# Sums of x for a Strassen product, read from x's copy in memory; one gate pair in place of two single gates; GELU's cubic factor in one pass

## The chip, the core and the metric

The kernel runs on one core of one Trainium2 chip. The metric is the time of one execution in microseconds of the device; lower is better. PE is the matrix engine, DVE the vector engine, ACT the engine of activation functions, POOL the general one; SP only issues transfers here, in the order of its program. Every engine works through a list of instructions that was fixed when the kernel was built.

## The reference

One step of a decoder layer, for 512 prompt tokens and 64 sample tokens, in fp32, D = 2048:

```
proj = x @ w_in + b_in                       # split into the branches' inputs and gates
y_s5 = gelu(s5(u));  y_s5 *= sigmoid(y_s5 @ w_glu + b_glu)
br_s5   = (y_s5 * silu(s5_z)) @ p_s5
br_gla  = (gla(q, k, v, a_low) * silu(gla_z)) @ p_gla
br_conv = (conv(ca, cb) * silu(cz)) @ p_conv
g_s5, g_gla, g_conv = split(sigmoid(gates))
out = (g_s5 * br_s5 + g_gla * br_gla + g_conv * br_conv) @ w_o
h = alpha * x + out;  h = h + sigmoid(h @ w_pg) * (p @ w_pe);  return layer_norm(h)
```

and the new states of the three branches. The S5 branch is a diagonal complex state-space model over 1024 channels. `gates` is 3 x 2048 columns wide: 48 columns of 128.

## The kernel before

All tensors lie transposed, features on partitions and the 576 tokens along the free axis. Each fp32 factor is split into a high part and a low part, both of which the matrix engine takes at full speed, and a product is made of three matmuls: high by high, high by low, low by high. The split is an ACT copy (high) and a DVE subtraction (low, L89). x is kept as 16 tiles `xh[k]` and 16 tiles `xl[k]`, 128 features each. All working tiles come from 71 slots of 128x576, called `sl`.

The input projection is a list of jobs. A *single job* is one column of 128 outputs: 16 k-tiles x 3 products x 2 halves of the tokens = 96 matmuls of 128x288 (L443). A *pair job* makes two columns by Strassen's scheme in Winograd's form: 7 products of 8 k-tiles x 3 matmuls, 168 in all (L472), and DVE and ACT join them. Two single jobs have 192. A pair's products take X's parts A11, A12, A22 and four sums S1 to S4 of x's quarters; with a = x[k] and b = x[k+8] (first half of the tokens 0, second 1):

```
S3 = a0 - a1;  S1 = a1 - b1;  S2 = S1 - a0;  S4 = b0 + S2
```

Order of the products: A11, S1, S2, S4, S3, A12, A22. The second one accumulates in the PSUM tile `aux`, the first and third in `mm`.

Order of the jobs: 8 columns of S5's input u, the column of a_low, then NFILL = 10 gates as single jobs, then the pairs (47), and so on. S5's work on its 8 blocks and the making of the sums run beside the first jobs as generators: each is stepped when it has credit, which a job's progress gives. When the column a_low is done, `make_forms` is started; it waits till 24 slots are free (10 once S5 is done), and makes the sums of one k after another from 16 adds of 128x576 (a = xh + xl, b likewise), subtractions and splits. The first pair needs all of them. A scheduler then fixes each engine's order by simulated times; it moves instructions of different generators past each other.

Of an S5 block the following is needed here. Its kernel `kd` is stored (L964) and loaded again in another layout by 16 DMAs (L980); the scan's input comes from PE (L998), the scan runs on DVE; `s5_out` joins both on PE (L1053 and L1057, the latter with the tiles loaded from kd), applies GELU and stores y by 8 DMAs (L1071). GELU is u times sigmoid of 1.596 u (1 + 0.044715 u^2): Square on ACT, factor and +1 (`ts`) and product (`mul`) on DVE, Sigmoid on ACT, product.

After each of the first eight gates, `x_out` writes two k-tiles of x to memory, `xd`: SP stores `xh[k]` (L1704) and POOL adds `xl[k]` to it by an accumulating DMA (L1705). x is needed there near the end of the layer, for alpha * x.

The file's line numbers are those of the profile of before; the changed file's are 10 or 11 higher from `make_forms` on.

Of the kernel before, what the change touches and what calls it, by code (L numbers as in the profile page):

```python
# [8 lines left out]
F32 = mybir.dt.float32  # L9
F32R = mybir.dt.float32r  # L10
I32 = mybir.dt.int32
AF = mybir.ActivationFunctionType
OP = mybir.AluOpType
# [13 lines left out]
UK = 8  # L27
# [10 lines left out]
TCK = dict(schedule_with_timeline_sim=True)  # L38
PRE, BLK_WAIT = 2, 4
OUT_WAIT, B_WAIT = 4, 2  # L40
NFILL = 10
AHEAD, PREP = 12.9, 6.5
RESERVE, BLOCK_SLOTS = 3, 13

# [1 line left out]
class K:  # L46
# [569 lines left out]
    def make_forms(self):  # L616

        S = {f: ([None] * UK, [None] * UK) for f in ("S1", "S2", "S3", "S4")}
        self.s3, self.stiles = [], []
        for k in range(UK):  # L620
            while len(self.free_slots) < (10 if "s5" in self.done else 24):
                yield None
            a, b, c = self.alloc(), self.alloc(), self.alloc()
            j = k % 2
            if j == 0:
                d, e = self.alloc(), self.alloc()
            cs = slice(j * H, j * H + H)
            self.add(a, self.xh[k].bitcast(F32), self.xl[k].bitcast(F32))
            self.add(b, self.xh[k + 8].bitcast(F32), self.xl[k + 8].bitcast(F32))
            self.sub(c[:, :H], a[:, H:], b[:, H:])  # L630
            self.sub(c[:, H:], c[:, :H], a[:, :H])
            yield 2.1
            self.add(d[:, cs], b[:, :H], c[:, H:])
            self.sub(e[:, cs], a[:, :H], a[:, H:])
            self.free(a, b)
            hi, lo = self.split(c)
            self.stiles += [hi, lo]
            self.free(c)
            for z, f in enumerate(("S1", "S2")):
                for t, p in zip((hi, lo), S[f]):  # L640
                    p[k] = t[:, z * H:(z + 1) * H]
            yield 1.5
            if j:
                hi, lo = self.split(d)
                self.stiles += [hi, lo]
                self.free(d)
                for z in range(2):
                    for t, p in zip((hi, lo), S["S4"]):
                        p[k - 1 + z] = t[:, z * H:(z + 1) * H]
                self.s3.append(e)  # L650
                yield 0.7
        for k in range(UK):
            for p, x in zip(S["S3"], (self.xh, self.xl)):
                p[k] = x[k][:, H:]
        x = (self.xh, self.xl)
        S["A11"] = tuple([t[:, :H] for t in p[:8]] for p in x)
        S["A12"] = tuple([t[:, :H] for t in p[8:]] for p in x)
        S["A22"] = tuple([t[:, H:] for t in p[8:]] for p in x)
        self.forms = S
        self.done.add("forms")  # L660
        yield 0.1
# [380 lines left out]
    def s5_out(self, b, st):  # L1042

        nc = self.nc
        hs = st.pop(("hs", b))
        U, cl, G, L = st.pop(("op", b))
        for _ in range(OUT_WAIT):
            yield
        p = self.two()
        for jj in range(4):  # L1050
            o = (jj // 2) * 512 + (jj % 2) * 144
            for pt in range(2):
                nc.tensor.matmul(p[:, o:o + 144], cl[pt][:, jj * 144 + 16:jj * 144 + 144], hs[pt][:, jj * 144:jj * 144 + 144],  # L1053
                                 start=pt == 0, stop=False)
            for h in range(2):
                gg = 2 * jj + h
                nc.tensor.matmul(p[:, o + h * 72:o + h * 72 + 72], L[gg // 4][:, (gg % 4) * 128:(gg % 4) * 128 + 128],  # L1057
                                 U[:, gg * 72:gg * 72 + 72], start=False, stop=h == 1,
                                 skip_group_check=h == 0)
        self.free(U, *cl, *L)  # L1060
        yield
        u, t = self.alloc(), self.alloc()
        self.act(self.s2(u), self.v2(p))
        self.act(self.s2(t), self.v2(p), AF.Square)
        self.ts(t, t, 0.044715, 1.0)
        self.mul(t, t, u)
        self.act(t, t, AF.Sigmoid, scale=2.0 * math.sqrt(2.0 / math.pi))
        self.mul(u, u, t)
        dst = self.yd[0, b].rearrange("(g c) (s n) -> s c g n", g=8, s=8)
        for s in range(8):  # L1070
            nc.sync.dma_start(dst[s], u[16 * s:16 * s + 16].rearrange("c (g n) -> c g n", g=8))  # L1071
        self.free(t)
        self.stored(u)
        yield 2.0
# [551 lines left out]
    def build(self):  # L1626
# [40 lines left out]
        def fill(n):  # L1667
            for _ in range(n):
                gate_one(*gates.popleft())
# [33 lines left out]
        def x_out(k):  # L1703
            self.pin(nc.sync.dma_start(self.xd[k], self.xh[k].bitcast(F32)))  # L1704
            nc.gpsimd.dma_start(self.xd[k], self.xl[k].bitcast(F32), accum_op=OP.add)  # L1705
# [3 lines left out]
        for n in range(8):  # L1709
            c = OFF["s5_u"] + n * 128  # L1710
            self.job(w_in, c, X, lambda ps, n=n: self.s5_store_u(n, ps))

        self.job(w_in, OFF["a"], X, evac_a, dual=3)
        for j in range(NFILL):
            fill(1)
            if j < 8:
                self.jobs[-1] = self.jobs[-1][:5] + (lambda j=j: (x_out(2 * j), x_out(2 * j + 1)),) + self.jobs[-1][6:]

        ys, yg, yz, yc, G, P = ([None] * 8, [None] * 8, [None] * 8, [None] * 8, [None] * 8, [])

# [589 lines left out]
```

## Time and profile before

| | |
|---|---|
| median of 3 runs | 2279.99 us (2278.43 to 2282.17) |
| profiled execution | 2280.14 us, span of the core 2278.1 us |
| mean granted clock of PE | 0.992 |
| PE busy | 2234.5 us (98%) |
| DVE busy | 1795.0 us (79%) |
| ACT busy | 1041.9 us (46%) |
| POOL busy | 69.3 us (3%) |
| first pair's first matmul | 338.25 us after the span's start |

The engines' busy times overlap, so each is to be read against the span alone. A wait stands in brackets at a row of a timeline: how long the engine was idle ahead of it, and what ended that. SP has no busy time; its rows are the issues of transfers, and a row's length is the time for issuing.

### The profile page before, as it was taken

Reading aid. Unit: us, or ns where it says so; the run is one execution under the profiler, and the core shown is the slowest. Engines: PE = TensorE matmul, PEld = TensorE weight load, DVE = VectorE, ACT = ScalarE, POOL = GpSimd, SP = SyncE. Lnnn points to the kernel's source line nnn. Section 1 sums busy time; section 2 is a strip of 40 time slices with the busy share of each in tenths; the row PEclk is TensorE's granted clock in tenths of the full one; section 3 lists DMA queues with packets and bytes.
Section 4 is the critical chain, followed back from the end, with each engine's and each line's share of the span. In section 5 each row is a group of like instructions: output and inputs, shape, how many; then the busy total and the mean of one; then the engine's idle time right before and its main releaser. Section 6 shows DMA issues by size and latency. Waiting matters only on the chain.

```text
span 2278.1 us, 44359 instructions
## 1 busy us (share of the span) xinstructions
PE 2234.5 (98%) x16892; PEld 2192.4 (96%) x16892; DVE 1795.0 (79%) x3417; ACT 1041.9 (46%) x2058; POOL 69.3 (3%) x121
## 2 busy tenths in 40 slices
PE   8998999999999999999999999999999999999998
PEld 7998999999999999999999999999989999999997
DVE  6977797999898999899989789856653777774556
ACT  4444445454545545545454556553432334453221
POOL 0000000000000000000000000000110000000000
PEclk9999999999999999999999999999999999999998
DMA  7567763434434444534444467856887444464322
GB/s 218 137 143 170 183 163 103 122 116 143 137 116 131 121 134 118 146 113 144 124 137 125 122 208 259 257 164 198 277 222 216 125 135 143 152 207 130 96 85 84
DMA packets 430005, 348.86 MB, mean 153 GB/s; under 512 B 51198, under 2 KB 368314, under 8 KB 429776
## 3 DMA queue, kind: packets, MB, share of 16 engines
q1 hardware_dynamic: 422336, 329.16, 48.7%
q0 software_dynamic: 7456, 16.88, 3.6%
q8 instruction: 132, 2.16, 0.4%
q14 instruction: 81, 0.66, 0.1%
HBM read 263.74 MB, written 82.89 MB: 152 GB/s over the span
## 4 chain that ended last, share of the span: by engine, by line
PE 85%; DMA 6%; DVE 4%; issue 2%; ACT 2%; SPq 1%; POOL 0%; DVEq 0%; ACTq 0%; POOLq 0%
PE mm L472 30%; PE mm L443 28%; PE aux L472 22%; DVE sl L89 2%; ACT sl L82 1%; PE mm L557 1%; DMA yd<-sl 1%; DMA sl<-gd 1%; PE aux L111 1%; PE two L111 1%; DMA xd<-sl 1%; DMA sl<-yd 1%; DVE lo L89 1%; DMA sl<-in_x_prompt 1%; PE two L1053 1%
## 5 line engine op out<-in xcount | busy, mean ns | idle before, releaser
L82 ACT ACTIVATE hi<-raw 128x512 fp32r<-128x512 f32 x800 | 501.4, 630 | 646.6 <-PE mm L443 247.5
L443 PE MATMUL mm<-sl,hi 128*128 128x288 f32 (+2 forms) x4000 | 726.7, 301 | 6.2 <-ACT sl L82 4.2
L472 PE MATMUL mm<-sl,hi 128*128 128x288 f32 x3520 | 710.1, 296 | 4.8 <-ACT sl L82 2.6
L89 DVE TENSOR_TENSOR lo<-raw,hi 128x512 fp32r<-128x512 f32 x796 | 544.2, 685 | 208.5 <-ACT hi L82 202.8
L443 PEld LDWEIGHTS mm<-sl,hi 128*128 128x128 f32 x4000 | 597.3, 190 | 12.7 <-ACT sl L82 5.0
L472 PEld LDWEIGHTS mm<-sl,hi 128*128 128x128 f32 x3520 | 564.8, 188 | 6.2 <-ACT sl L82 3.3
L472 PE MATMUL aux<-sl,hi 128*128 128x288 f32 x2640 | 528.2, 294 | 0.3 <-ACT hi L82 0.3
L472 PE MATMUL mm<-sl,lo 128*128 128x288 f32 x1760 | 518.3, 295 | 0.0
L89 DVE TENSOR_TENSOR sl<-sl,sl 128x576 f32<-128x576 f32 (+12 forms) x680 | 367.8, 577 | 97.1 <-ACT sl L82 43.5
L443 PE MATMUL mm<-sl,lo 128*128 128x288 f32 (+2 forms) x1968 | 433.4, 299 | 0.0
L472 PEld LDWEIGHTS aux<-sl,hi 128*128 128x128 f32 x2640 | 421.9, 188 | 0.7 <-ACT hi L82 0.6
L472 PE MATMUL aux<-sl,lo 128*128 128x288 f32 x1320 | 388.4, 294 | 0.0
L472 PEld LDWEIGHTS mm<-sl,lo 128*128 128x128 f32 x1760 | 330.7, 188 | 0.1
L443 PEld LDWEIGHTS mm<-sl,lo 128*128 128x128 f32 x1968 | 321.3, 190 | 2.6 <-issue 1.4
L472 PEld LDWEIGHTS aux<-sl,lo 128*128 128x128 f32 x1320 | 247.9, 188 | 0.1
L89 DVE TENSOR_TENSOR raw<-raw,sl 128x512 f32<-128x512 f32 x330 | 222.1, 683 | 5.3 <-DMA sl<-in_w_in 4.6
L82 ACT ACTIVATE sl<-sl 128x576 fp32r<-128x576 f32 (+11 forms) x291 | 127.0, 464 | 150.1 <-DVE sl L89 82.5
L82 ACT ACTIVATE hi<-sl 128x512 fp32r<-128x512 f32 x228 | 140.0, 628 | 104.2 <-PE mm L472 77.4
L89 DVE TENSOR_TENSOR lo<-sl,hi 128x512 fp32r<-128x512 f32 x228 | 154.8, 686 | 41.6 <-ACT hi L82 40.6
L107 DVE SCALAR_TENSOR_TENSOR sl<-sl,cw,sl 128x512 f32<-128x512 f32 x240 | 178.7, 745 | 0.3
L82 ACT ACTIVATE sl<-aux 128x288 f32<-128x288 f32 (+10 forms) x205 | 69.9, 354 | 55.0 <-PE aux L111 28.1
L82 ACT ACTIVATE sl<-mm 128x288 f32<-128x288 f32 (+3 forms) x146 | 65.8, 451 | 61.1 <-PE mm L472 32.5
(186 smaller groups left out, 1194.1 us busy)
## 6 DMA issues: line engine op xcount, KB each, us to landing
raw<-in_w_in SPq DMA_DIRECT2D x128, 512.0 KB
sl<-in_w_in SPq DMA_DIRECT2D x196, 256.0 KB
raw<-in_w_pg SPq DMA_DIRECT2D x32, 512.0 KB
gd<-sl SPq DMA_DIRECT2D x48, 288.0 KB
sl<-gd SPq DMA_DIRECT2D x48, 288.0 KB
raw<-in_p_s SPq DMA_DIRECT2D x16, 512.0 KB
raw<-in_p_conv SPq DMA_DIRECT2D x16, 512.0 KB
raw<-in_p_gla SPq DMA_DIRECT2D x16, 512.0 KB
```

The costliest lines, as they stand in the source:

```text
L82: return self.nc.scalar.activation(out, in_, func, **kw)
L89: self.nc.vector.tensor_tensor(out, a, b, op)
L107: self.nc.vector.scalar_tensor_tensor(out, a, s, b, op0=op0, op1=op1)
L111: self.nc.tensor.transpose(out, in_, self.ident[:n, :n])
L443: nc.tensor.matmul(ps[:, o:o + n], lh[:, k - ka], rh[k][:, c:c + n], start=a, stop=b)
L472: nc.tensor.matmul(ps[bank], lh[:, k - ka], rh[k], start=bool(a), stop=b, skip_group_check=not opens)
L557: nc.tensor.matmul(ps[:, o:o + m], lh[:, j], rh[k][:, c:c + m], start=a, stop=b)
L1053: nc.tensor.matmul(p[:, o:o + 144], cl[pt][:, jj * 144 + 16:jj * 144 + 144], hs[pt][:, jj * 144:jj * 144 + 144], start=pt == 0, stop=False)
```

## The change

Three edits and what hangs on them. Two gates fewer run as single jobs; they become one pair more (48 in place of 47). `make_forms` takes a and b as 32-bit tiles loaded from `xd`, one k ahead, in place of the 16 adds; that needs two slots more ahead of time, and its gates and credits are changed. `x_out` writes tiles j and j + 8 after gate j, so that both halves of a k are there. In GELU, ACT's Square takes the factor in as the square root of 0.044715, and one DVE pass makes (t + 1) * u.

```diff
-NFILL = 10
+NFILL = 8
...
         self.s3, self.stiles = [], []
+        ld = {}
+
+        def load(k):
+            if k < UK:
+                ld[k] = self.alloc(), self.alloc()
+                for z in range(2):
+                    self.nc.sync.dma_start(ld[k][z], self.xd[k + 8 * z])
+        while len(self.free_slots) < 24 and "s5" not in self.done:
+            yield None
+        load(0)
+        yield None
         for k in range(UK):
-            while len(self.free_slots) < (10 if "s5" in self.done else 24):
+            while len(self.free_slots) < (8 if "s5" in self.done else 24):
                 yield None
-            a, b, c = self.alloc(), self.alloc(), self.alloc()
+            load(k + 1)
+            a, b = ld.pop(k)
+            c = self.alloc()
...
-            self.add(a, self.xh[k].bitcast(F32), self.xl[k].bitcast(F32))
-            self.add(b, self.xh[k + 8].bitcast(F32), self.xl[k + 8].bitcast(F32))
             self.sub(c[:, :H], a[:, H:], b[:, H:])
             self.sub(c[:, H:], c[:, :H], a[:, :H])
-            yield 2.1
+            yield 0.8
...
-        self.act(self.s2(t), self.v2(p), AF.Square)
-        self.ts(t, t, 0.044715, 1.0)
-        self.mul(t, t, u)
+        self.act(self.s2(t), self.v2(p), AF.Square, scale=math.sqrt(0.044715))
+        self.stt(t, t, 1.0, u, OP.add, OP.mult)
...
-                self.jobs[-1] = self.jobs[-1][:5] + (lambda j=j: (x_out(2 * j), x_out(2 * j + 1)),) + self.jobs[-1][6:]
+                self.jobs[-1] = self.jobs[-1][:5] + (lambda j=j: (x_out(j), x_out(j + 8)),) + self.jobs[-1][6:]
```

What moves on SP: the queue around the last S5 block (block 7). Before, from kd's store of block 7 on (`sl_3553` and `sl_3554` are the tiles that its 16 loads fill in turn; a row of each is shown):

```order
L964 DMA kd<-sl_3432 128x128
L980 DMA sl_3553<-kd 16x4x128
L980 DMA sl_3554<-kd 16x4x128
...
L1663 DMA gd<-sl_3810 128x576
L383 DMA raw<-in_w_in 128x8x128 x2
L1071 DMA yd<-sl_3758 16x8x72 x8
L1663 DMA gd<-sl_4022 128x576
```

and with the change (L975 is kd's store, L991 its loads, L626 the loads of x for the sums, L1081 the stores of y of block 6, L1673 a gate's store):

```order
L975 DMA kd<-sl_3426 128x128
L1714 DMA xd<-sl_96 128x576
L991 DMA sl_3547<-kd 16x4x128
L991 DMA sl_3548<-kd 16x4x128
...
L1673 DMA gd<-sl_3803 128x576
L626 DMA sl_3966<-xd 128x576
L626 DMA sl_4010<-xd 128x576
L626 DMA sl_3950<-xd 128x576
L626 DMA sl_3951<-xd 128x576
L626 DMA sl_3967<-xd 128x576
L360 DMA raw<-in_w_in 128x4x256 x2
L1081 DMA yd<-sl_3752 16x8x72 x8
L626 DMA sl_3981<-xd 128x576
```

Five loads of x now stand behind the 16 loads of kd, and five more behind the 8 stores of block 6's y; four loads stand ahead of them, and the last two behind loads of weights.

On DVE, at the end of block 7's scan (`sl_1065` is the state it hands to PE, `sl_1058` the final state). Before, the sums' rows behind it read x's tiles, which have been there since the start:

```order
L89 TENSOR_TENSOR sl_1065<-sl_3713 64x4x63 x2
L89 TENSOR_TENSOR sl_1058<-sl_3713 128x4
L89 TENSOR_TENSOR sl_4125<-sl_93,sl_109 128x576
L89 TENSOR_TENSOR sl_3960<-sl_3960,sl_3958 128x288
L89 TENSOR_TENSOR lo<-raw,hi 128x512
L89 TENSOR_TENSOR sl_3758<-sl_3758,sl_3759 128x576
L89 TENSOR_TENSOR sl_3985<-sl_82,sl_98 128x576
```

With the change they read the loaded tiles:

```order
L89 TENSOR_TENSOR sl_1065<-sl_3707 64x4x63 x2
L89 TENSOR_TENSOR sl_1058<-sl_3707 128x4
L89 TENSOR_TENSOR sl_3972<-sl_3966 128x288
L107 SCALAR_TENSOR_TENSOR sl_3753<-sl_3753,sl_3752 128x576
L89 TENSOR_TENSOR sl_4016<-sl_4010 128x288
L89 TENSOR_TENSOR sl_3972<-sl_3950 128x288
L89 TENSOR_TENSOR lo<-raw,hi 128x512
L89 TENSOR_TENSOR sl_3752<-sl_3752,sl_3753 128x576
```

The row with `sl_3966` waits for the first load behind kd's; the last row shown is the product of GELU of block 6 (its tile `sl_3752` is what the 8 stores of y take), and stands five rows behind the wait. The row with `sl_3981`, the first load behind those stores, comes 12 rows further on.

On PE, block 7's output (L1053 and L1057, now L1064 and L1068). Before:

```order
L443 MATMUL mm<-sl_82,hi 128x288
L1053 MATMUL two<-sl_1065,sl_3427 128x144
L1057 MATMUL two<-sl_3237,sl_3553 128x72 x2
```

and with the change:

```order
L443 MATMUL mm<-sl_90,hi 128x288
L443 MATMUL mm<-sl_106,hi 128x288 x2
L443 MATMUL mm<-sl_90,lo 128x288 x2
L1064 MATMUL two<-sl_1065,sl_3421 128x144
L1068 MATMUL two<-sl_3232,sl_3547 128x72 x2
```

Between the scan's input for block 7 and these rows stand 43 gate matmuls fewer than before. Behind them stand 132 of gates (66 rows of two), and then the first pair.

## The prediction

> **What bounds the kernel now.** I read first the page's busy times and its chain of waits by engine, then the windows by stage, and then, in the stage that the change touches, the waits and the timelines of PE, DVE and SP.
>
> ```profile
> PE 2234.5 (98%) x16892; PEld 2192.4 (96%) x16892; DVE 1795.0 (79%) x3417; ACT 1041.9 (46%) x2058; POOL 69.3 (3%) x121
> ...
> PE 85%; DMA 6%; DVE 4%; issue 2%; ACT 2%; SPq 1%; POOL 0%; DVEq 0%; ACTq 0%; POOLq 0%
> ```
>
> ```profile
> 0.00:300.00 300.00, 283.88 (x2325) 268.84 (x2326) 234.95 (x600) 133.35 (x357) 19.10 (x35) 0.98 0.69 170
> 300.00:344.50 44.50, 44.50 (x338) 44.50 (x338) 40.27 (x78) 22.86 (x42) 2.34 (x4) 1.00 0.57 154
> 344.50:1403.00 1058.50, 1053.32 (x7912) 1050.57 (x7911) 948.57 (x1612) 542.15 (x1001) 13.05 (x30) 1.00 0.45 134
> ```
>
> The columns of a window are the time, then PE, PEld, DVE, ACT and POOL busy with their instructions, the granted clock and the DMA share. PE is the bound: from 344.5 us on, in the pairs, it is busy 1053 of 1058 us, at 1053.32 / 7912 = 0.1331 us per matmul. So time goes with the number of matmuls and with what PE has to wait for. It waits for nothing from 300 to 344.5 us, just where the sums of x are made (its last gates cover them), and DVE there works 40.3 of 44.5 us. That cover is what the change shortens.
>
> **Matmuls.** Two gates of 96 k-products, 192 matmuls, go; one pair of 168 comes. By the row above that is -192 x 0.1331 + 168 x 0.1331 = -25.6 + 22.4 = **-3.2 us**. But the 25.6 us go from ahead of the first pair and the 22.4 us are added behind it, so whatever the first pair has to wait for is seen in full.
>
> **When could the first pair run?** Before, it starts here, on PE (start, length of the row):
>
> ```profile
> 338.25 0.43 PE L472 MATMUL mm<-sl,hi 128*128 128x288 f32 x2
> ...
> 341.41 0.43 PE L472 MATMUL aux<-sl,hi 128*128 128x288 f32 x2
> ...
> 344.57 0.43 PE L472 MATMUL mm<-sl,hi 128*128 128x288 f32 x2
> ```
>
> The first product (X by A11) needs no sum; the second (aux, S1) needs S1 of every k; the third cannot pass the second. With 25.6 us of gates gone and no wait, the third would start at 344.6 - 25.6 = 319.0 us.
>
> **DVE up to that point.** Its timeline of before gives the start, when block 7's scan begins, and how closely it is packed; the groups of the same stretch give the prices.
>
> ```profile
> 278.71 0.42 DVE L89 TENSOR_TENSOR sl<-sl,sl 128x256 f32<-128x256 f32 x1 [3.73 <-PE two L998]
> ...
> 288.03 1.04 DVE L89 TENSOR_TENSOR sl<-sl 64x252 f32<-64x252 f32 x3
> 288.99 1.79 DVE L89 TENSOR_TENSOR sl<-sl,sl 128x576 f32<-128x576 f32 x3
> ...
> 304.72 0.76 DVE L89 TENSOR_TENSOR sl<-sl,sl 128x576 f32<-128x576 f32 x1 [1.11 <-DMA gd<-sl]
> ...
> 336.73 1.28 DVE L89 TENSOR_TENSOR raw<-raw,sl 128x512 f32<-128x512 f32 x2
> ```
>
> ```profile
> L89 DVE TENSOR_TENSOR lo<-raw,hi 128x512 fp32r<-128x512 f32 x24 | 16.4, 682 | 2.7 <-ACT hi L82 2.6
> L89 DVE TENSOR_TENSOR sl<-sl,sl 128x576 f32<-128x576 f32 x20 | 14.6, 749 | 1.1 <-DMA gd<-sl 1.1
> L89 DVE TENSOR_TENSOR sl<-sl,sl 128x288 f32<-128x288 f32 x24 | 10.3, 447 | 0.0
> L104 DVE TENSOR_SCALAR sl<-sl 128x576 f32<-128x576 f32 x3 | 1.4, 453 | 3.2 <-ACT sl L82 3.2
> ```
>
> The 16 removed adds of 128x576 are worth 16 x 0.749 = 12.0 us of DVE, rows overlapping by some 0.08 us, so 10.7 us of its time. Without any wait, in the changed order, DVE runs from the scan's first row to the first product of x it must wait for in about the time it took before from 278.71 to 288.99 (the scan, three lo's; 9.7 us by the shapes, to 288.4); then 17 rows up to the last lo ahead of the second batch of loads (9 of 288, 6 of 576, 2 of 512 columns: 4.0 + 4.5 + 1.4 = 9.9, less overlaps 8.7 us); then 48 rows up to S1's lo of k = 6 (25 of 288, 8 of 576, 15 of 512: 11.2 + 6.0 + 10.2 = 27.4, less overlaps 23.7 us). That is 42 us, to 320.8: about PE's 319.0. So the removed adds would just pay for the lost cover, if the loads that replace them came in time.
>
> **They come late: the queue.** SP issues in order, and the order puts the loads that DVE needs next behind the 16 loads of kd for block 7, and the following ones behind the 8 stores of yd of block 6, which wait for DVE itself. SP's rows of before at this place:
>
> ```profile
> 280.13 1.60 SPq L964 DMA_DIRECT2D kd<-sl  x1
> 286.24 8.80 SPq L980 DMA_DIRECT2D sl<-kd  x16
> 295.13 0.37 SPq L1663 DMA_DIRECT2D gd<-sl  x1
> 295.60 1.14 SPq L383 DMA_DIRECT2D raw<-in_w_in  x2
> 297.42 4.60 SPq L1071 DMA_DIRECT2D yd<-sl  x8
> ```
>
> The issues of kd end at 295.0, the gate's store at 295.5; the first late load is issued at 295.6 and not before. How long a load of 288 KB takes to land the chain of waits shows at other places, with the longest store to xd:
>
> ```profile
> 192.57 9.80 DMA xd<-sl
> ...
> 1465.02 5.27 DMA sl<-gd
> ...
> 1608.40 6.32 DMA sl<-gd
> 1614.79 4.49 DMA sl<-gd
> ```
>
> I take 5.3 (the middle of the three loads), bounds 4.5 and 9.8. DVE, at the load's user by 288.4, sits until 295.6 + 5.3 = 300.9: **12.5 us**. Six rows later (3.1 us, 304.0) it makes the product that the 8 yd stores wait for; these take 4.6 us of SP (to 308.6), then the second batch is issued and lands by 308.6 + 0.4 + 5.3 = 314.3, while DVE is through with its 17 rows at 300.9 + 8.7 = 309.6: **4.7 us** more. The last two loads wait for slots that DVE frees only some 5 us ahead of their use, so each load's 5.3 us plus issue is late by 1; I put **2 us** for both. S1's lo of k = 6 ends at 314.3 + 23.7 + 2 = 340.0 us, and the third product starts then, instead of at 319.0: **+21.0 us**. In all DVE was to gain 10.7 and gives back 19.
>
> The Trainium skill, DMA: Bandwidth & Descriptors, section Latency and other measured facts, puts the fixed cost of a DMA at about 2 us, mostly the round trip to memory, less when memory is lightly loaded. An estimate for these loads from it (2 us, and 288 KB at the 211 GB/s of the last column of the window from 280 to 300 us, shown further below, 1.4 us) would be 3.4 us and not 5.3, which takes 3 x 1.9 = 5.7 us from the sum and gives 2291; the measured loads above are longer, and I go by them.
>
> **What is hidden in PE's wait.** Block 7's output matmuls need the same kd loads:
>
> ```profile
> 297.03 0.41 PE L1053 MATMUL two<-sl,sl 128*128 128x144 f32 x2
> 297.27 0.56 PE L1057 MATMUL two<-sl,sl 128*128 128x72 f32 x4
> ```
>
> Before, 43 gate matmuls more stood between the scan's input and these, so that PE met them 19 us after it. Now they come 11 us after it, about 290, and PE waits 7 us. This lies within the 21 us, not beside them, since 17.6 us of gates and two products of 3.2 us stand between them and the third product: 297.3 + 3.5 + 17.6 + 6.4 = 324.8, earlier than DVE's 340.0.
>
> **Clock.** After a wait PE is slow for a while:
>
> ```profile
> 208.54 0.42 PE L958 MATMUL aux<-sl,sl 128*32 128x128 f32 x8 [2.23 <-DVE sl L89]
> ...
> 210.79 1.16 PE L443 MATMUL mm<-sl,hi 128*128 128x288 f32 x4
> ...
> 215.59 0.69 PE L443 MATMUL mm<-sl,hi 128*128 128x288 f32 x4
> ```
>
> ```profile
> 200.00:220.00 20.00, 17.44 (x152) 16.53 (x151) 14.14 (x32) 8.02 (x23) 2.57 (x3) 0.91 0.87 185
> ...
> 280.00:300.00 20.00, 20.00 (x160) 19.97 (x160) 19.91 (x44) 7.16 (x13) 3.06 (x4) 1.00 0.85 211
> ```
>
> Four matmuls take 1.16 instead of 0.69 for about 3 us, with a granted clock of 0.91 in that window: 1.3 us lost after the last long wait: **+1.3**. Slow matmuls inside the long wait cost nothing.
>
> **The early part.** The order in which x goes to xd (j and j + 8), the removed adds and the shorter list of gates change what stands between the S5 blocks. Ahead of 240 us PE waits like this:
>
> ```profile
> PE two L998 <- ACT sl L82: 3.5, 3, 1.7
> PE aux L111 <- DMA sl<-in_s_c_re: 3.3, 1, 3.3
> ...
> PE aux L958 <- DVE sl L89: 2.5, 2, 2.2
> ```
>
> In the new order 17 to 25 gate matmuls, 2 to 3 us each time, stand ahead of some of these, so PE could gain up to 9 us there. But what counts is when SP gets to the kd loads and DVE to block 7, and those hang on the S5 chain, not on PE; I let **-2 us** through, bounds 0 and -9.
>
> **GELU.** One pass of 0.45 us and one of 0.75 become one of 0.75 (two operands), for 8 blocks: 3.6 us of DVE, six of them where DVE has slack (234.95 of 300 us) and two inside its waits. 0 us; if DVE were the limit throughout, -0.9. The 16 new issues of SP at 0.4 us are counted above.
>
> **Sum.** 2280.14 (the profiled execution, span 2278.1) - 3.2 + 21.0 + 1.3 - 2.0 = 2297.2. The profiled execution stands 0.15 us above the median, so 2297. From the pairs on all is shifted alike, PE being full there.
>
> **The rivals.** (1) *Loads in time.* If the early waits vanish and SP reaches block 7's kd loads 12 us sooner, both waits go. For it: 9 us of waits on PE, and DVE busy in 235 of the first 300 us only. Against it: the kd loads wait for the kd store (issued 280.13, loads from 286.24), which hangs on the S5 chain. Time: 2280.1 - 3.2 + 2 (DVE at 320.8) = 2279, or 2270 with all 9 us: faster or the same. (2) *Only the wait for kd.* If the scheduler's loads land early enough, say because the first are issued while SP waits for the kd store, PE's 324.8 instead of 319.0 counts: 2280.1 - 3.2 + 5.8 + 1.3 = 2284. Against it: SP is in order. (3) *Longer queueing.* Landings of 9.8 us, as at 192.57, in one batch, and no early gain: 2297.2 + 4.5 + 2 = 2304; in all three 2313.
>
> **How the numbers follow.** Forecast 0.62 (own range 2290, with all of the early gain, to 2304, with one landing of 9.8 us and no early gain), rival 1 0.12, rival 2 0.15, rival 3 0.11. Within 0.2% (about what a measurement of this kernel can tell from no change) is 2275.4 to 2284.6. Faster: two thirds of rival 1, 0.08. Same: the rest of it and 0.12 of rival 2, 0.16. Slower: 0.76. The range is 2280 to 2306: it takes in rival 2 and the short end of rival 3, and leaves out rival 1 and the longest landings, 0.17.
>
> **What would show it.** DVE idle some 12 us from about 288 us, released by a DMA from xd, and again about 5 us near 310; SP issuing those loads only behind block 7's 16 kd loads; PE idle for 5 to 8 us ahead of block 7's output matmuls, and in pieces in the first pair's second product, whose successor starts at 338 to 342; then 48 pairs without a wait, all later ones 17 us late. If DVE does not wait for xd, the forecast is wrong; if it does and the time is still under 2285, the early part gave more than I let through.

## The result, and the profile after

The changed kernel took 2296.43 us (median of 4 runs, 2295.28 to 2299.46) against 2279.93 us of the kernel before: a ratio of 1.0077, 95% interval 1.0063 to 1.0091. It is slower by 16.5 us; 2297 had been forecast. The profiled execution took 2296.91 us, span 2295.1.

The page's busy times and the windows by stage (time, then PE, PEld, DVE, ACT and POOL busy, the granted clock, the DMA share and GB/s) of the changed kernel:

```profile
PE 2235.8 (97%) x16868; PEld 2191.7 (95%) x16868; DVE 1791.9 (78%) x3410; ACT 1050.9 (46%) x2072; POOL 69.1 (3%) x121
```

```profile
0.00:300.00 300.00, 278.25 (x2271) 262.18 (x2271) 221.70 (x575) 128.85 (x351) 19.09 (x35) 0.98 0.69 174
300.00:344.50 44.50, 34.30 (x224) 33.28 (x223) 35.98 (x70) 21.43 (x40) 2.34 (x4) 0.86 0.61 179
344.50:1403.00 1058.50, 1058.17 (x7974) 1056.72 (x7975) 952.29 (x1618) 541.65 (x1002) 13.06 (x30) 1.00 0.45 132
```

PE has 24 matmuls fewer and is busy 1.3 us longer, because many of them ran at the slow clock (0.86 in the second window, 1.00 before). That window was full before; now PE idles in it for 10.2 us, and ahead of it for 5.6 us more than before. From 344.5 to 1403 us, in the pairs, nothing is wrong: PE is busier than before. So the loss lies where the first pair begins. PE there (a bracket is the idle time before the row and what ended it):

```profile
297.26 1.10 PE L1068 MATMUL two<-sl,sl 128*128 128x72 f32 x4 [7.16 <-DMA sl<-kd]
...
321.05 0.43 PE L472 MATMUL mm<-sl,hi 128*128 128x288 f32 x2
...
324.21 0.43 PE L472 MATMUL aux<-sl,hi 128*128 128x288 f32 x2
...
327.31 0.40 PE L472 MATMUL aux<-sl,hi 128*128 128x288 f32 x1 [2.02 <-DVE sl L89]
...
334.78 0.61 PE L472 MATMUL aux<-sl,hi 128*128 128x288 f32 x1 [5.75 <-ACT sl L82]
337.82 0.61 PE L472 MATMUL aux<-sl,hi 128*128 128x288 f32 x1 [2.43 <-DVE sl L89]
...
338.71 0.68 PE L472 MATMUL mm<-sl,hi 128*128 128x288 f32 x2
```

The pair's first product starts 17.2 us earlier than before (321.05 against 338.25); its second then waits for S1 of one k after the other, and the third starts at 338.71, only 5.9 us earlier than before (344.57). The gates taken away were 25.6 us long. DVE, which makes S1:

```profile
276.83 0.43 DVE L89 TENSOR_TENSOR sl<-sl,sl 128x256 f32<-128x256 f32 x1 [3.46 <-PE two L1009]
278.60 1.42 DVE L89 TENSOR_TENSOR sl<-sl,two 128x256 f32<-128x256 f32 x4 [1.34 <-DMA yd<-sl]
...
300.04 0.46 DVE L89 TENSOR_TENSOR sl<-sl 128x288 f32<-128x288 f32 x1 [10.53 <-DMA sl<-xd]
...
302.12 0.46 DVE L89 TENSOR_TENSOR sl<-sl 128x288 f32<-128x288 f32 x1 [0.59 <-DMA sl<-xd]
...
311.57 1.43 DVE L89 TENSOR_TENSOR sl<-sl,sl 128x576 fp32r<-128x576 f32 x2 [3.21 <-DMA yd<-sl]
...
329.31 1.29 DVE L89 TENSOR_TENSOR raw<-raw,sl 128x512 f32<-128x512 f32 x2 [0.47 <-DMA sl<-in_w_in]
```

and SP's queue, which the loads of x (L626) share with kd's loads (L991) and y's stores (L1081):

```profile
280.45 0.39 SPq L975 DMA_DIRECT2D kd<-sl  x1
...
286.95 9.14 SPq L991 DMA_DIRECT2D sl<-kd  x16
296.19 0.37 SPq L1673 DMA_DIRECT2D gd<-sl  x1
296.66 2.30 SPq L626 DMA_DIRECT2D sl<-xd  x5
299.01 4.59 SPq L360 DMA_DIRECT2D raw<-in_w_in  x2
303.88 4.54 SPq L1081 DMA_DIRECT2D yd<-sl  x8
308.53 3.83 SPq L626 DMA_DIRECT2D sl<-xd  x5
```

The first load behind kd's is issued at 296.66 and its user on DVE has sat since 289.5.

### The profile page after: what moved, and what is told of

The parts are those of the page before. It is cut to its first block, busy times and chain, and to the rows that moved or that the text cites. A ratio compares the mean times of both kernels' runs of the same rounds, so it can differ in the third digit from the quotient of the medians.

```text
span 2295.1 us, 44333 instructions
## 1 busy us (share of the span) xinstructions
PE 2235.8 (97%) x16868; PEld 2191.7 (95%) x16868; DVE 1791.9 (78%) x3410; ACT 1050.9 (46%) x2072; POOL 69.1 (3%) x121
## 4 chain that ended last, share of the span: by engine, by line
PE 83%; DMA 6%; DVE 4%; issue 2%; SPq 2%; ACT 2%; POOL 0%; DVEq 0%; ACTq 0%; POOLq 0%
PE mm L472 30%; PE mm L443 25%; PE aux L472 23%; DVE sl L89 2%; ACT sl L82 1%; PE two L111 1%; PE aux L111 1%; DMA raw<-in_w_in 1%; DVE lo L89 1%; PE mm L557 1%; DMA sl<-zd 1%; DMA sl<-yd 1%; DVE sl L107 1%; DMA yd<-sl 1%; ACT L82 1%
## 5 line engine op out<-in xcount | busy, mean ns | idle before, releaser
L472 PE MATMUL mm<-sl,hi 128*128 128x288 f32 x3584 | 724.8, 297 | 2.3 <-DVE sl L89 1.3
L443 PE MATMUL mm<-sl,hi 128*128 128x288 f32 (+2 forms) x3872 | 701.4, 300 | 7.1 <-ACT sl L82 3.4
L472 PE MATMUL aux<-sl,hi 128*128 128x288 f32 x2688 | 539.1, 295 | 10.7 <-ACT sl L82 5.7
L472 PE MATMUL mm<-sl,lo 128*128 128x288 f32 x1792 | 529.1, 296 | 0.0
L472 PEld LDWEIGHTS aux<-sl,hi 128*128 128x128 f32 x2688 | 430.1, 188 | 12.1 <-ACT sl L82 6.0
L89 DVE TENSOR_TENSOR sl<-sl,sl 128x576 f32<-128x576 f32 (+11 forms) x656 | 353.6, 572 | 111.8 <-ACT sl L82 38.2
L443 PE MATMUL mm<-sl,lo 128*128 128x288 f32 (+2 forms) x1904 | 420.1, 299 | 0.0
L472 PEld LDWEIGHTS mm<-sl,lo 128*128 128x128 f32 x1792 | 338.0, 189 | 0.1
L82 ACT ACTIVATE sl<-sl 128x576 fp32r<-128x576 f32 (+10 forms) x291 | 127.2, 464 | 141.4 <-DVE sl L89 80.8
L82 ACT ACTIVATE sl<-aux 128x288 f32<-128x288 f32 (+9 forms) x206 | 69.9, 354 | 60.8 <-PE aux L111 28.7
```

The costliest lines, as they stand in the source:

```text
L82: return self.nc.scalar.activation(out, in_, func, **kw)
L89: self.nc.vector.tensor_tensor(out, a, b, op)
L443: nc.tensor.matmul(ps[:, o:o + n], lh[:, k - ka], rh[k][:, c:c + n], start=a, stop=b)
L472: nc.tensor.matmul(ps[bank], lh[:, k - ka], rh[k], start=bool(a), stop=b, skip_group_check=not opens)
```

## The experiments

Between the start of the first pair's third product and the end of the span lie 1933.5 us before (47 pairs) and 1956.4 us after (48 pairs). So the time of each kernel can be read roughly from when that product starts; the rest varies by 5 to 7 us among kernels with the same number of pairs. The table has, of each profiled execution, that start, the rest of the span, and the measured ratio to the kernel before.

| kernel | third product starts | rest of span | ratio, 95% interval |
|---|---|---|---|
| before | 344.57 | 1933.5 | 1 |
| the change | 338.71 | 1956.4 | 1.0077 [1.0063, 1.0091] |
| eight gates, adds, new GELU and order of x's stores | 338.96 | 1956.9 | 1.0086 [1.0072, 1.0099] |
| the change with ten gates | 351.28 | 1931.6 | 1.0018 [1.0008, 1.0027] |
| loads of x on POOL's queue | 336.72 | 1956.2 | 1.0078 [1.0066, 1.0091] |
| no loads, no adds | 328.50 | 1959.3 | 1.0035 [1.0024, 1.0046] |
| kd taken early | 335.31 | 1955.7 | 1.0070 [1.0057, 1.0084] |
| kd early and loads on POOL | 332.41 | 1962.2 | 1.0070 [1.0057, 1.0082] |
| before, new GELU alone | 349.56 | 1931.5 | 1.0014 [1.0005, 1.0023] |
| before, new order of x's stores alone | 344.88 | 1931.9 | 0.9996 [0.9986, 1.0006] |
| before, eight gates alone | 338.07 | 1955.5 | 1.0078 [1.0064, 1.0093] |
| no loads, no adds, old GELU | 324.15 | 1955.5 | 1.0024 [1.0015, 1.0034] |
| the change, old GELU | 333.45 | 1957.3 | 1.0067 [1.0053, 1.0082] |
| loads and order of x's stores, ten gates, old GELU | 351.87 | 1928.4 | 1.0017 [1.0008, 1.0026] |

In two rows the start is not the end of the second product: without loads and adds, and in the change with the old GELU, PE's order has two matmuls of the third product ahead of the second's last ones, and the others follow at 333.61 and 335.84.

The theory: the time is set by when S1 is complete, against how far two gates fewer have brought PE. The rivals: that the loads as such, or the wait for kd, or an added pair as such are the loss.

**The loads taken back: eight gates with the adds.**

```diff
...
-            load(k + 1)
-            a, b = ld.pop(k)
-            c = self.alloc()
+            a, b, c = self.alloc(), self.alloc(), self.alloc()
...
+            self.add(a, self.xh[k].bitcast(F32), self.xl[k].bitcast(F32))
+            self.add(b, self.xh[k + 8].bitcast(F32), self.xl[k + 8].bitcast(F32))
...
```

What else hangs on the loads (their helper, the slots asked for, the credit) is as before too.

> The change with its loads of x taken back: the sums are made from the two parts by 16 adds of DVE again, with eight single gates, the new order of x's stores and the new GELU. Theory (what the first pair waits for sets the time): no wait for x, and block 7's output again has 40 gate matmuls ahead of it, so no wait for kd; but DVE needs 54 us from the scan's first row (278.6) to S1's last lo, 332.6, so the third product starts near 333 instead of 319. 2280.1 - 3.2 + 13.6 + 1.3 - 2 = 2290 us. Rival A (the loads are the whole loss): 2277. Rival B (the wait for kd alone decides, whatever makes the sums): 2277 too, as that wait is gone. Rival C (the shorter cover alone, loads or adds alike): 2296.

Measured: 2299.06 us, 9 more than the theory's number. DVE's work after the scan's first row was as reckoned, without a wait:

```profile
258.77 0.76 DVE L107 SCALAR_TENSOR_TENSOR sl<-sl,sl 128x576 f32<-128x576 f32 x1 [10.16 <-ACT sl L82]
...
282.16 0.43 DVE L89 TENSOR_TENSOR sl<-sl,sl 128x256 f32<-128x256 f32 x1 [3.58 <-PE two L998]
...
336.78 1.43 DVE L89 TENSOR_TENSOR sl<-sl,sl 128x576 fp32r<-128x576 f32 x2 [0.30 <-ACT sl L82]
```

From 282.16 to S1's last low parts are 54.6 us. But the scan started 3.5 us later than before, since DVE had sat 10.2 us at GELU's one pass in an earlier block (first row). Rivals A and B (2277) are refuted: loads and adds bring the third product to the same time, 338.7 and 339.0. Rival C (the shorter cover alone, 2296) comes nearest. This run had the new GELU in it, so the gates were also tried by themselves.

**Two gates fewer and nothing else.**

```diff
-NFILL = 10
+NFILL = 8
```

> The kernel before with eight single gates and 48 pairs; sums by adds, GELU and x's stores as before. All runs so far end 1956 to 1957 us after the start of the first pair's third product with 48 pairs, 1932 to 1934 with 47; the time is 2 us more. Theory (DVE's work up to S1 against PE's cover, and nothing else): the scan starts as before at 278.7, DVE needs 55 us to S1's last lo, third product near 334.5, time 2293 us. Without the early wait on ACT that the run with adds, eight gates and the new GELU had, so about 4 to 6 us less than its 2299. Rival (removing gates costs nothing by itself, the loads and GELU cost all): 2277.

Measured: 2294.93 us (expected 2293; third product at 338.07, expected 334.5, of which 1.7 us is a later scan). The slowdown of the change is there in full, with no load of x for the sums and no edit to GELU. Its DVE and PE:

```profile
280.43 0.43 DVE L89 TENSOR_TENSOR sl<-sl,sl 128x256 f32<-128x256 f32 x1 [3.70 <-PE two L998]
...
335.89 1.43 DVE L89 TENSOR_TENSOR sl<-sl,sl 128x576 fp32r<-128x576 f32 x2 [0.31 <-ACT sl L82]
```

```profile
321.09 0.40 PE L472 MATMUL aux<-sl,hi 128*128 128x288 f32 x1 [2.87 <-DVE sl L89]
...
329.70 0.61 PE L472 MATMUL aux<-sl,hi 128*128 128x288 f32 x1 [8.08 <-ACT sl L82]
```

DVE has no wait between 280.43 and 335.89: it is full for 55 us, and PE stands in the second product. So eight gates are too short a cover for the sums as made before.

**The loads with the cover of ten gates.**

```diff
-NFILL = 8
+NFILL = 10
```

> The change with ten single gates and 47 pairs as before, loads of x kept. Theory: DVE waits for x as in the change (10 and 3 us) and has S1 near 338, but PE is not there before 341, so this wait is hidden. The wait for kd, 7.2 us and 2 us of slow clock, stays, since only 12 gate matmuls stand between the two last pieces of S5 and block 7's output; PE is full from there on, so it is seen: third product near 351 instead of 344.6, 2280 + 7 - 2 = 2285 us. Rival A (two gates of cover hide everything): 2278 to 2280. Rival B (the loads' traffic slows all): over 2290.

Measured: 2282.36 us (expected 2285). PE does not wait in the first pair; DVE's waits for x (7.20 and 2.48 us, until 298.7 and 302.2) and for a store of y (1.71 us, until 309.9) are hidden. The third product starts 6.7 us later than before, behind other waits of PE: the longest are 3.7 us for kd (7.2 had been expected) and 4.2 us, until 202.6, for ACT.

**The loads on POOL's queue.**

```diff
-                    self.nc.sync.dma_start(ld[k][z], self.xd[k + 8 * z])
+                    self.nc.gpsimd.dma_start(ld[k][z], self.xd[k + 8 * z])
```

> The change with the 16 loads of x issued by POOL's queue in place of SP's. Theory with slots: the first batch comes near 293 to 297 instead of 300 to 302, but the second batch needs the slot that block 7's output frees on PE at 303, itself late by kd's loads, so it lands near 309.5 instead of 313 and DVE has S1 near 331; third product near 332 instead of 338.7, 2290 us. Rival A (SP's queue alone makes the loads late): no wait for x, the third product right behind the first two, near 327, 2283 us. Rival B (landing times or traffic, not the queue): as the change, 2296.

Measured: 2298.31 us, where 2290 was expected. DVE and PE:

```profile
295.17 0.46 DVE L89 TENSOR_TENSOR sl<-sl 128x288 f32<-128x288 f32 x1 [3.65 <-DMA sl<-xd]
...
307.18 1.50 DVE L89 TENSOR_TENSOR sl<-sl,sl 128x288 f32<-128x288 f32 x3 [7.35 <-PE two L1064]
```

```profile
301.33 1.13 PE L1068 MATMUL two<-sl,sl 128*128 128x72 f32 x4 [9.44 <-DMA sl<-kd]
```

The first wait fell from 10.5 to 3.7 us and ended 4.9 us sooner (295.17 instead of 300.04), so SP's queue was indeed part of what made it; for 2 us of the fall DVE only came later, having waited for ACT in the scan. But a wait of 7.4 us took its place, for what block 7's output on PE frees, and that output came later (301.3 instead of 297.3): kd's loads took 10.9 us to issue instead of 9.1, and the rest of the 4 us lies between the last issue and the landing. The third product gained 2.0 us, the profiled execution 2.2 (2294.71); over the runs nothing is left.

**No loads and no adds.** The sums are made from the high parts of x alone.

```diff
...
-            load(k + 1)
-            a, b = ld.pop(k)
+            a, b = (self.xh[z].bitcast(F32) for z in (k, k + 8))
...
```

> The change without its loads and without the adds: the sums are made from the high parts of x alone (their low parts are left out, so the sums are less exact). Theory: nothing to wait for; DVE has S1 near 319; block 7's output has 42 gate matmuls ahead of it again; third product near 321. 2280.1 - 3.2 + 1.8 - 1 = 2278 us. This is the most that the change could have given. Rival (one pair more costs more than two gates, or the early order costs): over 2285.

Measured: 2287.77 us, 10 more than expected. Here too DVE and ACT had waited earlier, at GELU (8.21 us at 269.35 on DVE), and the scan started at 287.0 instead of 278.7. With the old GELU beside it:

```diff
-        self.act(self.s2(t), self.v2(p), AF.Square, scale=math.sqrt(0.044715))
-        self.stt(t, t, 1.0, u, OP.add, OP.mult)
+        self.act(self.s2(t), self.v2(p), AF.Square)
+        self.ts(t, t, 0.044715, 1.0)
+        self.mul(t, t, u)
```

> The change without loads and without adds (sums from x's high parts alone, less exact), and with GELU's old two passes. Theory: the run without loads was late by 9.4 us of ACT waiting for a slot ahead of GELU of block 6, which the new GELU's order brings; with the old one the scan starts near 279, DVE has S1 42 us later at 321, PE is there at 324: third product near 324, 2282 us. Rival (the early wait comes with eight gates, whatever GELU is): 2287 to 2289 as before.

Measured: 2283.25 us; the third product started at 324.15 (expected 324), straight behind the first two. Without the cost of adds or loads, eight gates are still 0.24% slower than ten with the adds. PE has other waits there, 2.7 us ahead of block 7's output and 3.4 us in three waits for ACT ahead of S5's transposes; that they are the whole difference was not tested.

**Block 7's loads without their wait.** They read block 6's kd, so that this block's output is computed with the wrong matrix; the transfers are the same. Then the same with the loads of x on POOL's queue.

```diff
-        src = self.kd[b].rearrange("(g c) w -> c g w", g=8)
+        src = self.kd[min(b, 6)].rearrange("(g c) w -> c g w", g=8)
```

> The change with block 7's 16 loads taken from block 6's kd, which has long been stored (so block 7's output is computed with the wrong kernel matrix): the same transfers, without the wait for kd's own store. Theory: SP gets through them by about 286 instead of 296, PE's wait of 7.2 us ahead of block 7's output goes, the first batch of loads of x lands near 297 instead of 300 to 302, the second (still behind the 8 stores of y) near 309 instead of 313; third product near 334 instead of 338.7, 2292 us. Rival A (PE's wait for kd is what costs): all 7 us of it and 2 of slow clock come back, third product near 329, 2287. Rival B (neither matters, DVE's work alone): 2296.

> Both at once: block 7's loads from block 6's kd (its output is wrong) and the loads of x on POOL's queue. Theory: nothing is left of the queue, of kd's round trip and of the slot that block 7's output holds; DVE needs 41 to 44 us from 278 on, PE is there at 320; third product near 324, 2282 us. Rival (landing time and traffic set the loads, not the queue and the slot): as with POOL's queue alone, 2296 to 2298.

Measured: 2293.96 us for the first (expected 2292, third product 334; found 335.31). Time and start came near, but PE's wait ahead of block 7's output did not go: DVE and PE of the first:

```profile
293.51 1.41 DVE L89 TENSOR_TENSOR sl<-sl 128x288 f32<-128x288 f32 x4 [6.50 <-DMA sl<-xd]
```

```profile
294.78 0.84 PE L1064 MATMUL two<-sl,sl 128*128 128x144 f32 x2 [6.25 <-DVE sl L89]
```

In place of kd, PE waited 6.3 us for DVE, which had stood in its wait for x. So this run does not show what the wait for kd alone costs.

The second was expected at 2282 and took 2294.09. POOL and DVE of the second:

```profile
287.32 0.54 POOL L626 DMA_DIRECT2D sl<-xd  x1 [0.46 <-DMA sl<-kd]
297.39 0.89 POOL L1715 DMA_DIRECT2D xd<-sl  x1 [9.53 <-DMA xd<-sl]
297.96 1.95 POOL L626 DMA_DIRECT2D sl<-xd  x3
```

```profile
303.79 0.46 DVE L89 TENSOR_TENSOR sl<-sl 128x288 f32<-128x288 f32 x1 [9.58 <-DMA sl<-xd]
```

The expectation had overlooked POOL's own order: ahead of three loads stood x_out's accumulating transfer, waiting 9.5 us for SP's store of the same tile, and the loads waited behind it. The queue had changed, not the waiting in it. The third product came at 332.41, but the rest of the span is 5.8 us longer than in the change: PE idles 30.9 us there instead of 27.4 and is busy 2.3 us longer, without one wait that stands out (the longest is 3.9 us). Why is open.

**GELU alone, the order of x's stores alone, and the change without its GELU.** The kernel before with one edit each; the diffs are those of the change. The change with the old GELU has the diff shown above.

> The kernel before with the new GELU alone. Theory: one DVE pass fewer for each of 8 blocks lies beside other work: 2279 to 2280 us, no difference beyond 0.1%.

> The kernel before with the new order of x's stores alone (j and j + 8 after gate j). Theory: the same number of transfers at the same places: 2279 to 2280 us, no difference beyond 0.1%.

> The change with GELU's old two passes. Theory: the waits for the loads of x and for kd stay as they are (10 and 3 us on DVE, 7 on PE): third product 338 to 340, 2296 to 2298 us, the same as the change within 0.1%. Rival (the new GELU costs 3 us here as it did alone): 2293.

Measured: 2282.0, 2278.45 and 2293.44 us. The order of x's stores does nothing. GELU by itself costs 0.14% (interval 0.05% to 0.23%), against the expectation. Its ACT, DVE and PE:

```profile
259.09 1.19 ACT L82 ACTIVATE sl<-two 128x576 f32<-128x576 f32 x2 [9.17 <-DMA raw<-in_w_in]
```

```profile
260.31 0.76 DVE L107 SCALAR_TENSOR_TENSOR sl<-sl,sl 128x576 f32<-128x576 f32 x1 [10.45 <-ACT sl L82]
```

```profile
260.33 2.19 PE L998 MATMUL two<-sl,sl 128*64 128x72 f32 x32 [5.41 <-ACT sl L82]
```

The two ACT rows are GELU's copy and Square of an earlier block. They now stand ahead of work that PE needs, and wait 9.2 us; before they stood further back and waited 1.8 (first row below). In the changed kernel that wait is not there either (second row). DVE behind them sits 10.5 us, PE 5.4. The pass saved is 0.45 us. What holds the ACT rows back (the releaser named is a load of weights; in two other runs a store of y) was not settled; a slot that y's stores have yet to free fits both but wasn't tried by itself.

```profile
255.00 1.19 ACT L82 ACTIVATE sl<-two 128x576 f32<-128x576 f32 x2 [1.80 <-DMA yd<-sl]
```

```profile
253.01 1.19 ACT L82 ACTIVATE sl<-two 128x576 f32<-128x576 f32 x2 [2.59 <-DMA yd<-sl]
```

So in the change the new GELU must cost its time elsewhere. The change with the old GELU did not keep the waits that had been expected of it. SP issues kd's store for block 7 at 269.83 (280.45 in the change), and PE waits only 1.2 us ahead of block 7's output, and DVE's wait for x comes in pieces; two of them are:

```profile
295.37 0.46 DVE L89 TENSOR_TENSOR sl<-sl 128x288 f32<-128x288 f32 x1 [2.21 <-DMA sl<-xd]
...
300.19 0.46 DVE L89 TENSOR_TENSOR sl<-sl 128x288 f32<-128x288 f32 x1 [3.08 <-DMA sl<-xd]
```

From 276 us on DVE waits there 10.6 us for x and 1.5 us for stores of y, against 11.1 and 4.5 us in the change. The rival's time, 2293, was right.

**The loads with ten gates and the old GELU.**

```diff
-NFILL = 8
+NFILL = 10
```

> The change with ten single gates and GELU's old two passes, so that only the loads of x and the order of its stores are left of it. Theory: with the cover of ten gates DVE's waits for x are hidden, and without the new GELU the early wait on ACT (4.2 us at 202.6 with ten gates and the new GELU) goes; about 3 us less than that run's 2282, so 2279, no difference from before within 0.2%. Rival (the loads cost something by their own, cover or not: PE's wait for kd stays in full): 2282 to 2285.

Measured: 2282.3 us, the rival's time, though not by the wait for kd that it names. The early wait on ACT did not go either (4.5 us, until 208.8). The third product started at 351.87. DVE and PE ahead of block 7's output:

```profile
291.03 1.50 DVE L89 TENSOR_TENSOR sl<-sl,sl 128x288 f32<-128x288 f32 x4 [5.36 <-DMA sl<-xd]
```

```profile
293.44 0.82 PE L1064 MATMUL two<-sl,sl 128*128 128x144 f32 x2 [4.61 <-DVE sl L89]
```

With ten gates the sums are hidden either way, but a row that waits for a load of x stands among the last rows of the scan, whose result PE needs: by the chain of waits a load issued at 278.15 landed 12.8 us later, DVE waited 5.4 us for it and PE 4.6 us for DVE.

No version beat the kernel before.

## Why the prediction was right

*Matmuls.* -25.6 and +22.4 us: 24 fewer were counted. The rest of the span behind the third product is longer by 22.9 us, where 22.4 for the pair and 1.3 for the clock had been put.

*DVE.* The scan began 1.9 us earlier (276.83); the load's user was reached at 289.5 (predicted 288.4), after a wait of 1.3 us for a store of y.

*The loads.* First load behind kd's issued at 296.66 (predicted 295.6), wait 10.5 us to 300.04 (12.5 to 300.9). It landed within 3.4 us of its issue, not 5.3. The estimate from the Trainium skill (DMA: Bandwidth & Descriptors, Latency and other measured facts) was 3.4, and the trace agrees with it for this load. DVE's next wait for a load ended at 302.12; by the chain of waits that load took 4.5 us from 297.63.

*The second wait* was 3.2 us (4.7 predicted) and ended by the landing of y's stores, which by the profile read the slot that the low parts of S1 and S2 go to. The prediction had the load behind the stores as its end. It is the same queue with another last link. *The third*, for the last two loads, did not come; DVE waited 0.5 us for a load of weights. In all DVE waited 15 us from 289 us on, not 19.2. Along the path: the first wait ended 0.9 us sooner than forecast, the second 2.7 us sooner (311.57, forecast 314.3); the way from there to the last low part, at about 338, was 0.7 us longer than forecast, and the third product began 0.7 us behind that, at 338.71 (340.0, or 338.0 with the 2 us of the early part taken off).

*PE's wait for kd:* 7.16 us, until 297.26 (7, until 297.3), and hidden as said. The slow rows behind it made the first product start at 321.05 instead of 318.4, also hidden.

*Clock.* The third product's 24 matmuls took 5.4 us instead of 3.2, the first 20 of them 0.24 us apart instead of 0.13, with a granted clock of 0.51 from 334.7 to 343.7 us: 2.2 us, predicted 1.3.

*The early part*, put at -2 us, did not come through where it was to count. The scan began 1.9 us earlier, but SP issued kd's store at 280.45 (280.13 before) and its loads from 286.95 on (286.24 before). So the loads of x went out later, not earlier: with the 2 us taken off, 293.6 had been forecast, and 296.66 was measured. Of the three edits named for this term, the order of x's stores gives nothing alone, and eight gates alone start the scan 1.7 us later. That the sum came out within 1 us all the same is in part luck: this gain failed to come, and the waits were shorter by about as much.

*GELU* at 0 us was wrong as a term. By itself it costs 3 us, and taken out of the change it gives back 3.0 us (2293.44 against 2296.43; the intervals 1.0053 to 1.0082 and 1.0063 to 1.0091 overlap, so this is not clear of noise). The cost is not that of its instruction but of the order that comes with it, and not the same order in both kernels: alone, ACT's wait of 9.2 us; in the change, the later kd store and longer waits of DVE. The sum could hold without such a term because its waits were read from the order of the changed kernel, in which the new GELU already stood. This reason is argued, not tested.

*And the weight of the causes.* That the late loads give back what the removed adds bring was in the prediction (10.7 against 19). The runs showed more plainly what this means: with loads or adds, eight gates alone give the whole slowdown. What rival 1 (loads in time) would give, the run without loads and adds and with the old GELU shows most nearly: 2283, not 2279. That this is also close to rival 2's number, 2284, is chance, as there was no load of x to wait for. Rival 3, longer landings, had no part in the changed kernel (3.4 and 4.5 us), but with ten gates and the old GELU one load took 12.8 us.

## What to carry to other kernels

Work that hides another engine's preparation is worth its own time and that preparation's time: before shortening it, add up the preparation from the last event that it depends on, and compare ends. A load in place of arithmetic is only as early as what stands in front of it in its queue (here 16 loads, and DVE idle for 10.5 us), and moving it to another engine's queue helps only if nothing waits there and its slot is free. After such an edit read the order of the neighbours: one instruction fewer can move another engine's waiting instruction ahead of what the bound engine needs.

## What had not been expected

Saving one of two passes of 0.45 and 0.75 us on DVE made the kernel 3 us slower, with a wait of ACT, 1.8 us before and 9.2 after, that the new order brought. POOL, busy 3%, was no free queue: three loads stood 9.5 us behind a transfer waiting for a store. And the loads cost something by themselves: with ten gates and the old GELU the kernel is 0.17% slower although no wait for x holds up the first pair. One such wait reaches PE earlier, ahead of block 7's output (4.6 us); how much of the 0.17% is its share was not tried.
